# Weight parts moved 32 bytes further into their buffers in a one-core hybrid decoder layer

## The chip, the core and the metric

The kernel runs on one core of a Trainium2 chip. The time is device microseconds (us) of one execution; of the kernel before, three runs were timed. A profile of one further execution gives the rows below. Engines are named as in the profile: PE is the matrix engine's matmuls and PEld its weight loads, DVE the vector engine, ACT the scalar engine, POOL GpSimd, and SP the queue that issues the loads.

## What is computed

One layer of a decoder trunk over 256 tokens of width 2048, all in float32. The normalised tokens `xn` go through one wide input projection (22,852 columns); its columns feed four branches of width 1024. Each branch is gated, projected back to 2048 columns, weighted by a sigmoid gate and summed:

```python
[a_q, a_k, a_v, a_g, c_b, c_c, c_h, c_g, s_q, s_k, s_v, s_g, m_q, m_g,
 i_q, i_k, i_w, r_a, r_c, r_s, r_m] = [xn @ w for w in cols]
...
merged = (sigmoid(r_a) * (y_a @ w_branch[0]) + sigmoid(r_c) * (y_c @ w_branch[1])
          + sigmoid(r_s) * (y_s @ w_branch[2]) + sigmoid(r_m) * (y_m @ w_branch[3]))
return x + merged @ w_out          # and a last RMSNorm
```

The branches are a block attention, a short convolution, a sparse attention with an indexer, and an attention into 256 memory tokens. Nearly all the work is the projections: 256 tokens times some 254 MB of weights, each weight used for 256 tokens and then never again.

## The kernel before

A float32 product is made of three matmuls in the one-pass format `float32r`. Every operand is split into a rounded part `hi` and the rest `lo` (line 106: ACT casts to `hi`, DVE subtracts to get `lo`), and the product is hi·hi + hi·lo + lo·hi.

Weights arrive in 1 MB loads (`raw`, 128 partitions of 8 KB). Each load is split in two halves of 1024 columns (`split_weights`, line 117, and `quarter_parts`, line 188), and each half gets one pair of buffers `hi` and `lo` from `parts_tiles` (line 113). The pool `spl` has four buffers for `hi` and four for `lo`, used in turn, so a pair is rewritten four halves later. This is **the ring**. A buffer holds 1024 + 16 floats, 4160 bytes of each partition. 4160 is 16 times 256 plus 64, so the four buffers of a ring start 64 bytes apart modulo 256. In the addresses of the built program the ring is used in the order 0, 192, 128, 64, 0, ... bytes modulo 256 (`hi` and `lo` of a pair alike). The token tiles that meet these weights on the matrix engine (`x_hl`, `m16a`, `m16b`, `x_sums`, `y`, `mt`) all start at 0 modulo 256, and all slices of tokens and weights are multiples of 512 bytes, so a matmul's weights stand against its tokens at the ring's offset.

Two forms of matmul use the ring:

- **The 256-column form** (`products_t`, lines 141 to 143): 128 weight columns are loaded into the array (the stationary operand), and the 256 tokens stream past (the moving operand). A half of a load feeds 24 such matmuls (4 slices of k, 2 blocks of columns, 3 products).
- **The 512-column form** (`products`, lines 162 to 164): 128 tokens are loaded, and 512 weight columns stream past. A half feeds 12 such matmuls where both halves of the tokens use it (2 slices of k, 2 token halves, 3 products), and 6 where one does. The last two blocks of the output projection are 256 columns wide and also have the weights moving.

While a matmul streams its moving operand, the engine loads the stationary operand of the next one, so two streams are read from the same memory at a time. Some value and gate projections (`by_halves`, line 225) save a product of blocks by sums and differences of weight quarters, which DVE makes before the split. The order of the work is the program's own order, as a scheduler places it; nothing in it depends on an address.

Of the kernel before, what the change touches and what calls it, by code (L numbers as in the profile page):

```python
# [10 lines left out]
F32R = mybir.dt.float32r  # L11
# [4 lines left out]
P = 128  # L16
# [4 lines left out]
NB = 512  # L21
# [27 lines left out]
def hybrid_kernel(ctx, tc, x, xT, mem, memT, ln_g, mem_ln_g, w_t, w_n, w_idx, conv_w, conv_b, w_mem_k, w_mem_v,  # L49
# [7 lines left out]
    spl = ctx.enter_context(tc.tile_pool(name="spl", bufs=4))  # L57
# [53 lines left out]
        return rawp.tile([P, 4 * NB], F32, name="raw", tag="raw").rearrange("p (k c) -> p k c", c=c)  # L111

    def parts_tiles(w=NB, c=NB):
        return [spl.tile([P, 2 * NB + 16], F32R, name=n, tag=n)[:, :2 * NB].rearrange("p (k c) -> p k c", c=w)[:, :, :c]
                for n in ("hi", "lo")]

    def split_weights(src, w):

        c = src.shape[2]
        per, half = 4 * NB // w, 2 * NB // w  # L120
        for k0 in range(0, src.shape[1], per):
            raw = raw_tile(w)[:, :, :c]
            nc.sync.dma_start(out=raw, in_=src[:, k0:k0 + per])
            for h0 in range(0, per, half):
                hi, lo = parts_tiles(w, c)
                split(hi, lo, raw[:, h0:h0 + half])
                for k in range(half):
                    yield hi[:, k], lo[:, k], k0 + h0 + k
# [59 lines left out]
    def quarter_parts(raw):  # L188
        for h in (0, 2):
            hi, lo = parts_tiles()  # L190
            split(hi, lo, raw[:, h:h + 2])
            for i in range(2):
                yield hi[:, i], lo[:, i], h + i
# [131 lines left out]
    def to_heads(name, c0):  # L325

        dst = big.tile([P, 8, T], F32, name=name, tag=name)
        for b in range(4):
            copy_t(dst[:, 2 * b:2 * b + 2], project_t(w_t[FIRST[c0] + b], x_act))
        return dst  # L330
# [176 lines left out]
    def first_columns(dst):  # L507

        src = w_t[FIRST[M_Q]:FIRST[M_Q] + 2].rearrange("b p k c -> p k b c")
        outs = [bank("first", tag)[:, :T] for tag in "aabb"]  # L510
        xraw = big.tile([P, KC, T], F32, name="xraw", tag="m16b")
        for k0 in range(0, KC, 4):
            raw = raw_tile(NB).rearrange("p k (b c) -> p k b c", b=2)
            n = 1 if k0 == 0 else 2
            for k in range(k0, k0 + 4, n):
                nc.sync.dma_start(out=xraw[:, k:k + n], in_=xT[:, k:k + n])
                for i in range(n):
                    nc.sync.dma_start(out=raw[:, k + i - k0], in_=src[:, k + i])
                for i in range(n):
                    if (k + i) % 2 == 0:  # L520
                        hi, lo = parts_tiles(NB, NB)
                    split_tokens(xraw[:, k + i], k + i, g_x, x_hl[:, k + i])
                    h, lw = hi[:, (k + i) % 2], lo[:, (k + i) % 2]
                    split(h, lw, raw[:, k + i - k0].rearrange("p b c -> p (b c)"))
                    for j in range(4):
                        js = slice(j * P, (j + 1) * P)
                        products_t(outs[j], h[:, js], lw[:, js], k + i, KC, x_act)
        copy_t(dst[:, 0:4], outs)
# [40 lines left out]
    k = big.tile([P, 8, T], F32, name="kt", tag="kt")  # L569
# [28 lines left out]
    k = to_heads("kt", S_K)  # L598
# [6 lines left out]
    k = to_heads("kt", A_K)  # L605
# [111 lines left out]
```

## Time and profile before

| | |
|---|---|
| median of 3 runs | 1406.79 us (1406.69 to 1406.96) |
| profiled execution | 1407.13 us, its span in the trace 1405.4 us |
| PE busy | 1389.9 us, 99% |
| weight loads (PEld) busy | 1247.0 us, 89% |
| DVE busy | 933.1 us, 66% |
| ACT busy | 728.0 us, 52% |
| granted matrix clock | 0.999 of full speed |
| loads from HBM | 265.9 MB, mean 191 GB/s |

Matmuls are pipelined: a row's duration reaches into the next one's, so a busy share of 99% only says that something is always in flight. What a matmul costs in a row of matmuls is the distance from its start to the next one's start, which is read from the timeline. A start there is given to 0.01 us; over 12 or 24 matmuls the mean distance is known to a nanosecond.

### The profile page before, as it was taken

To read this page: it belongs to the slowest core of one execution; us is meant where nothing else is said; L and a number is where in the kernel's file an instruction comes from. 1 tells how busy PE (TensorE), PEld (TensorE's weight loads), DVE (VectorE), ACT (ScalarE), POOL (GpSimd) and SP (SyncE) were. 2 spreads that over 40 slices of the span, in tenths; PEclk is the share of its full clock that TensorE was granted. 3 is DMA by queue.
4 is the path that set the end of the run, shared out by engine and by line. 5 is a ranking of instruction groups with operands and counts; after the bars stand their busy time and mean duration, and the time that the engine had idled before them with its cause. 6 is when DMAs were issued, how large, how long until landed. Compare 5 with 4: busy or idle time off the path is not lost.

```text
span 1405.4 us, 21264 instructions
## 1 busy us (share of the span) xinstructions
PE 1389.9 (99%) x8796; PEld 1247.0 (89%) x8796; DVE 933.1 (66%) x1123; ACT 728.0 (52%) x991; POOL 11.2 (1%) x26
## 2 busy tenths in 40 slices
PE   9999999999999999999999999999999999999997
PEld 9998998779999898877999899877999998778887
DVE  6686764774757885487546886487547558787654
ACT  7664675453445585445444585445343345545443
POOL 1000000000000000000000000000000000000000
PEclk9999999999999999999999999999999999999999
DMA  9774545375553735537554645537555654736551
GB/s 343 287 260 165 206 150 180 120 269 163 187 183 121 266 128 185 197 120 243 204 184 150 239 146 188 192 114 266 200 184 182 225 194 155 265 120 240 185 200 65
DMA packets 49969, 269.49 MB, mean 192 GB/s; under 512 B 6656, under 2 KB 17456, under 8 KB 19024
## 3 DMA queue, kind: packets, MB, share of 16 engines
q1 hardware_dynamic: 48960, 264.03, 54.6%
q0 software_dynamic: 624, 3.31, 0.6%
q8 instruction: 69, 1.13, 0.3%
q10 hardware_dynamic: 288, 0.79, 0.1%
q14 instruction: 28, 0.23, 0.0%
HBM read 265.88 MB, written 2.10 MB: 191 GB/s over the span
## 4 chain that ended last, share of the span: by engine, by line
PE 85%; DVE 9%; issue 2%; DMA 2%; ACT 2%; SPq 0%; POOLq 0%; POOL 0%; DVEq 0%; ACTq 0%
PE acc L143 13%; PE acc L141 13%; PE acc L142 13%; DVE lo L108 5%; PE w L163 4%; PE w L164 4%; PE w L162 4%; PE r L163 3%; PE r L164 3%; PE r L162 3%; PE o L163 2%; PE o L162 2%; PE o L164 2%; DMA raw<-in_w_n 1%; PE y L163 1%
## 5 line engine op out<-in xcount | busy, mean ns | idle before, releaser
L108 DVE TENSOR_TENSOR lo<-raw,hi 128x1024 fp32r<-128x1024 f32 (+1 forms) x538 | 639.7, 1203 | 427.2 <-ACT hi L107 425.9
L107 ACT CAST hi<-raw 128x1024 fp32r<-128x1024 f32 (+1 forms) x538 | 550.8, 1030 | 558.0 <-PE acc L142 201.5
L142 PE MATMUL acc<-x_hl,hi 128*128 128x256 f32 x1520 | 426.5, 281 | 0.0
L143 PE MATMUL acc<-x_hl,lo 128*128 128x256 f32 x1520 | 425.9, 280 | 0.0
L141 PE MATMUL acc<-x_hl,hi 128*128 128x256 f32 x1520 | 425.3, 280 | 0.0
L141 PEld LDWEIGHTS acc<-x_hl,hi 128*128 128x128 f32 x1520 | 286.6, 189 | 0.3
L143 PEld LDWEIGHTS acc<-x_hl,lo 128*128 128x128 f32 x1520 | 286.4, 189 | 0.1
L142 PEld LDWEIGHTS acc<-x_hl,hi 128*128 128x128 f32 x1520 | 286.1, 188 | 0.3
L163 PE MATMUL w<-lo,y 128*128 128x512 f32 x256 | 100.7, 393 | 0.0
L164 PE MATMUL w<-hi,y 128*128 128x512 f32 x256 | 100.6, 393 | 0.0
L162 PE MATMUL w<-hi,y 128*128 128x512 f32 x256 | 100.6, 393 | 0.0
L163 PE MATMUL r<-lo,x_hl 128*128 128x512 f32 x248 | 97.5, 393 | 0.0
L164 PE MATMUL r<-hi,x_hl 128*128 128x512 f32 x248 | 97.4, 393 | 0.0
L162 PE MATMUL r<-hi,x_hl 128*128 128x512 f32 x248 | 97.4, 393 | 0.0
L162 PEld LDWEIGHTS w<-hi,y 128*128 128x128 f32 x256 | 48.1, 188 | 11.1
L163 PEld LDWEIGHTS w<-lo,y 128*128 128x128 f32 x256 | 48.0, 188 | 11.0
L164 PEld LDWEIGHTS w<-hi,y 128*128 128x128 f32 x256 | 48.1, 188 | 10.9
L162 PEld LDWEIGHTS r<-hi,x_hl 128*128 128x128 f32 x248 | 46.6, 188 | 10.5
L163 PEld LDWEIGHTS r<-lo,x_hl 128*128 128x128 f32 x248 | 46.5, 188 | 10.5
L164 PEld LDWEIGHTS r<-hi,x_hl 128*128 128x128 f32 x248 | 46.6, 188 | 10.4
L163 PE MATMUL o<-lo,mt 128*128 128x512 f32 (+1 forms) x160 | 55.6, 348 | 0.0
L164 PE MATMUL o<-hi,mt 128*128 128x512 f32 (+1 forms) x160 | 55.5, 348 | 0.0
(247 smaller groups left out, 1865.9 us busy)
## 6 DMA issues: line engine op xcount, KB each, us to landing
raw<-in_w_t SPq DMA_DIRECT2D x92, 1024.0 KB, 5.0
raw<-in_w_n SPq DMA_DIRECT2D x80, 1024.0 KB, 4.9
raw<-in_w_branch SPq DMA_DIRECT2D x32, 1024.0 KB, 5.2
raw<-in_w_out SPq DMA_DIRECT2D x16, 1024.0 KB, 4.8
raw<-in_w_mem_k SPq DMA_DIRECT2D x8, 1024.0 KB, 5.8
raw<-in_w_mem_v SPq DMA_DIRECT2D x8, 1024.0 KB, 4.9
raw<-in_w_t SPq DMA_DIRECT2D x16, 256.0 KB, 5.4
raw<-in_memT SPq DMA_DIRECT2D x2, 1024.0 KB, 7.6
```

Of the source, the lines that this page charges most:

```text
L107: nc.scalar.copy(out=hi, in_=src)
L108: nc.vector.tensor_sub(out=lo, in0=src, in1=hi.bitcast(F32))
L141: nc.tensor.matmul(o, lhsT=hi, rhs=a[:, 0], start=(k == 0), stop=False)
L142: nc.tensor.matmul(o, lhsT=hi, rhs=a[:, 1], start=False, stop=False)
L143: nc.tensor.matmul(o, lhsT=lo, rhs=a[:, 0], start=False, stop=(k == nk - 1))
L162: nc.tensor.matmul(o, lhsT=ah, rhs=hi, start=start, stop=False)
L163: nc.tensor.matmul(o, lhsT=ah, rhs=lo, start=False, stop=False)
L164: nc.tensor.matmul(o, lhsT=al, rhs=hi, start=False, stop=stop)
```

## The change

Each buffer of the ring keeps its size of 1024 + 16 floats, and the used part of it starts 8 floats (32 bytes) later. The four offsets modulo 256, in the order of use, become 32, 224, 160, 96. The built program has the same instructions in the same order on every engine; only addresses differ.

```diff
     def parts_tiles(w=NB, c=NB):
-        return [spl.tile([P, 2 * NB + 16], F32R, name=n, tag=n)[:, :2 * NB].rearrange("p (k c) -> p k c", c=w)[:, :, :c]
+        return [spl.tile([P, 2 * NB + 16], F32R, name=n, tag=n)[:, 8:8 + 2 * NB].rearrange("p (k c) -> p k c", c=w)[:, :, :c]
                 for n in ("hi", "lo")]
```

## Rows read from the trace of the kernel before

**Rows 1.** The page's busy time of each engine with its share of the span and its instructions, and the matrix clock in 40 slices (9 is 90% or more).
```profile
PE 1389.9 (99%) x8796; PEld 1247.0 (89%) x8796; DVE 933.1 (66%) x1123; ACT 728.0 (52%) x991; POOL 11.2 (1%) x26
...
PEclk9999999999999999999999999999999999999999
```

**Rows 2.** Groups of PE instructions, shapes apart: line, engine, operation, result<-operands, weight rows*columns, moving shape, count | busy us, mean ns | idle us before. Lines 141 and 162 only; lines 142 and 143, and 163 and 164, have as many.
```profile
L141 PE MATMUL acc<-x_hl,hi 128*128 128x256 f32 x1504 | 420.8, 280 | 0.0
...
L162 PE MATMUL w<-hi,y 128*128 128x512 f32 x256 | 100.6, 393 | 0.0
...
L162 PE MATMUL r<-hi,x_hl 128*128 128x512 f32 x248 | 97.4, 393 | 0.0
...
L162 PE MATMUL o<-hi,mt 128*128 128x512 f32 x96 | 37.7, 393 | 0.0
...
L162 PE MATMUL m<-hi,x_sums 128*128 128x512 f32 x84 | 33.7, 401 | 1.1 <-ACT hi L107 1.1
...
L162 PE MATMUL x<-hi,x_hl 128*128 128x512 f32 x84 | 33.1, 395 | 0.0
L162 PE MATMUL y<-hi,x_hl 128*128 128x512 f32 x84 | 33.1, 394 | 0.0
...
L162 PE MATMUL z<-hi,x_hl 128*128 128x512 f32 x56 | 22.2, 397 | 0.0
...
L141 PE MATMUL acc<-m16a,hi 128*128 128x256 f32 x64 | 18.0, 281 | 0.0
...
L141 PE MATMUL acc<-m16b,hi 128*128 128x256 f32 x64 | 17.8, 279 | 0.0
...
L162 PE MATMUL o<-hi,mt 128*128 128x256 f32 x64 | 17.8, 281 | 0.0
...
L141 PE MATMUL first<-x_hl,hi 128*128 128x256 f32 x64 | 16.3, 290 | 0.7 <-ACT hi L107 0.7
...
L162 PE MATMUL v<-hi,m16a 128*128 128x512 f32 x32 | 12.6, 394 | 0.0
...
L162 PE MATMUL v<-hi,m16b 128*128 128x512 f32 x32 | 12.2, 392 | 0.0
...
L162 PE MATMUL z<-hi,x_sums 128*128 128x512 f32 x28 | 11.0, 393 | 0.0
L162 PE MATMUL m<-hi,x_hl 128*128 128x512 f32 x28 | 11.0, 393 | 0.0
...
L141 PE MATMUL acc<-x_hl,hi 128*68 128x256 f32 x16 | 4.5, 278 | 0.0
```

**Rows 3.** Timeline of PE (start us, duration us) in a stretch of the 256-column form: the first matmul with each pair of the ring, at offsets 192, 128, 64, 0 and 192 again; 24 matmuls from one to the next.
```profile
392.85 0.28 PE L141 MATMUL acc<-x_hl,hi 128*128 128x256 f32 x1
...
395.57 0.28 PE L141 MATMUL acc<-x_hl,hi 128*128 128x256 f32 x1
...
398.41 0.28 PE L141 MATMUL acc<-x_hl,hi 128*128 128x256 f32 x1
...
401.15 0.28 PE L141 MATMUL acc<-x_hl,hi 128*128 128x256 f32 x1
...
404.03 0.28 PE L141 MATMUL acc<-x_hl,hi 128*128 128x256 f32 x1
```

**Rows 4.** The same in a stretch of the 512-column form: the first matmul with the pairs at 64, 0, 192, 128 and 64 again, 12 matmuls from one to the next, and between the second and the third the start of the seventh matmul of the pair at 0.
```profile
252.15 0.39 PE L162 MATMUL w<-hi,y 128*128 128x512 f32 x1
...
254.90 0.39 PE L162 MATMUL w<-hi,y 128*128 128x512 f32 x1
...
256.28 0.39 PE L162 MATMUL w<-hi,y 128*128 128x512 f32 x1
...
257.64 0.39 PE L162 MATMUL w<-hi,y 128*128 128x512 f32 x1
...
260.44 0.39 PE L162 MATMUL w<-hi,y 128*128 128x512 f32 x1
...
263.23 0.39 PE L162 MATMUL w<-hi,y 128*128 128x512 f32 x1
```

**Rows 5.** The same in the indexer's last block, where a weight load has 68 columns instead of 128: the first matmul with the pairs at 128, 64, 0 and 192, and the first of what follows; 12 matmuls from one to the next.
```profile
342.21 0.28 PE L141 MATMUL acc<-x_hl,hi 128*68 128x256 f32 x1
...
343.62 0.28 PE L141 MATMUL acc<-x_hl,hi 128*68 128x256 f32 x1
...
345.01 0.28 PE L141 MATMUL acc<-x_hl,hi 128*68 128x256 f32 x1
...
346.41 0.28 PE L141 MATMUL acc<-x_hl,hi 128*68 128x256 f32 x1
...
347.83 0.28 PE L141 MATMUL acc<-x_hl,hi 128*128 128x256 f32 x1
```

**Rows 6.** Groups that write the ring, and one that writes the token parts, shapes apart; columns as in rows 2, with what ended the idle time.
```profile
L107 ACT CAST hi<-raw 128x1024 fp32r<-128x1024 f32 x518 | 539.7, 1048 | 548.3 <-PE acc L142 195.0 <-PE w L164 98.3 <-PE r L164 74.2
...
L107 ACT CAST x_hl<-xn 128x1024 fp32r<-128x1024 f32 x4 | 4.2, 1046 | 0.0
```

**Rows 7.** The same for DVE, and the one group of matmuls that waits for it.
```profile
L108 DVE TENSOR_TENSOR lo<-raw,hi 128x1024 fp32r<-128x1024 f32 x518 | 627.3, 1224 | 414.4 <-ACT hi L107 413.2
...
L163 PE MATMUL m<-lo,x_sums 128*128 128x512 f32 x84 | 33.8, 402 | 3.0 <-DVE lo L108 3.0
```

## The prediction

> **What bounds the kernel now.** I read the page first. PE is busy for 99% of the span and its clock is granted in full in all 40 slices [rows 1]: 1389.9 us of 1405.4 us, nothing else above 89%. So the time is the number of matmuls times the distance at which one follows another, plus small stalls. The groups of PE instructions give the numbers [rows 2]. The 256-column form with the ring's weights as stationary operand counts 1504 + 16 + 64 + 64 + 64 = 1712 on line 141, and as many on lines 142 and 143: 5136. The 512-column form counts 256 + 248 + 96 + 84 + 84 + 84 + 56 + 32 + 32 + 28 + 28 = 1028 on line 162, three times that is 3084. Another 3 x 64 = 192 are the output projection's 256-column blocks with moving weights. Attention has its own buffers, which the change leaves alone. In nearly all these groups the idle time before is zero: the matmuls follow one another without a wait, and what is left is the distance from start to start.
>
> Then the timeline, one turn of the ring at a time, because the change moves addresses and nothing else. In the 256-column form [rows 3] 24 matmuls take:
> - offset 192: 395.57 - 392.85 = 2.72 us, 113.3 ns each
> - offset 128: 398.41 - 395.57 = 2.84 us, 118.3 ns
> - offset 64: 401.15 - 398.41 = 2.74 us, 114.2 ns
> - offset 0: 404.03 - 401.15 = 2.88 us, 120.0 ns
>
> The code, shapes and line numbers are the same in all four; no wait lies between. What differs is where the weights stand against the tokens, so the address has a price, up to 6.7 ns on 113.3. In the 512-column form [rows 4] 12 matmuls take 2.75 us at 64 (229.2 ns), 2.74 us at 0 (228.3), 2.80 us at 192 (233.3) and 2.79 us at 128 (232.5). The pair at 0 starts slowly and ends at (257.64 - 256.28) / 6 = 226.7 ns. The order of the offsets is another one than in the first form: 192 is best there and worst here.
>
> One view tells how far the offset alone sets the price. In the indexer's last block the weight loads are shorter, 68 columns [rows 5], and 12 matmuls take 1.41, 1.39, 1.40 and 1.42 us at 128, 64, 0 and 192: 117.5, 115.8, 116.7 and 118.3 ns. The offset 192, the best with full loads, is the worst here. So the price is not a property of the offset but of how the two streams, the moving operand and the next weights, fall against each other in time; the offset only shifts one of them.
>
> **The change part by part.** It adds and removes no instruction. Three things read or write the shifted addresses.
>
> Writes by ACT and DVE: 518 casts of 1048 ns and 518 subtractions of 1224 ns [rows 6, 7]. The nearest row with another destination is the cast into the token parts, 1046 ns [rows 6]; I take no change. They are hidden by ACT's 548 us and DVE's 414 us of idle time, which ends mostly with PE freeing a buffer. The cover is thin only where block products wait for DVE, 3.0 us in all [rows 7]; if it went there, I would expect no more than as much again, 3 us.
>
> The loads of raw weights go elsewhere and are untouched.
>
> Reads by PE. No row shows a weight part at an odd multiple of 32, so I bound it by the distances the rows show. The mean over the ring is (404.03 - 392.85) / 96 = 116.5 ns in the first form and (263.23 - 252.15) / 48 = 230.8 ns in the second.
> - First form, low end: all four at 113.3 ns, -3.1 x 5136 = -16 us. High end: all at 120.0 ns, +3.5 x 5136 = +18 us.
> - Second form, low end: 226.7 ns, -4.1 x 3084 = -13 us. High end: 233.3 ns, +2.5 x 3084 = +8 us.
> - The 192 others: at most 6.7 ns each either way, 1.3 us, taken as nothing.
>
> What I take: each new offset lies halfway between two old ones, and averaged over the ring the neighbours' means give the old mean again. That is no change, in both forms. The mix with other phases [rows 5] gives (347.83 - 342.21) / 48 = 117.1 ns, 0.6 ns over the first form's mean, +3 us. Both are mixtures of good and bad phases and I see no reason to prefer one; the middle is +1.5 us. Against the profiled execution that is 1405.4 + 1.7 around the span + 1.5 = 1408.6; that execution lies 0.3 us over the median, so **1408 us**.
>
> One rule speaks against any effect. The trace shows 113.3 and 120.0 ns for the same instructions at two addresses. The Trainium skill, page "SBUF — State Buffer", section "Who interferes with whom", states that PE reads moving operand and weights through two independent ports and never waits on anyone. By that rule the four stretches would be equal and the change worth nothing, 1406.8 us; by the rows a shift can be worth up to 30 us. The measurement decides, and the rule stays as a rival only, the last one below.
>
> **The rivals.**
>
> *Locked apart (faster).* The two streams may settle so that they no longer meet. For it: distances in a stretch settle to one value and stay there, 113.3 or 120.0 [rows 3] and 226.7 [rows 4]; all four old offsets are multiples of 64 and so meet the tokens' reads on the same 64-byte steps, and half a step may avoid them. Against it: two of the four parts in the first form are free already, and the second form reverses the order. One form alone gives 1406.8 - 16 = 1391 or 1406.8 - 13 = 1394 us; both give 1378 us. DVE would then be late next, in the block products [rows 7].
>
> *Locked together (slower).* The place is the 256-column form, lines 141 to 143. There PEld, 89% busy over the span [rows 1], has little slack beside a matmul of 256 columns, so any beat that the load loses is the matmul's loss too. 32 bytes are half of a 64-byte step: each load of 512 bytes and each moving row then begins and ends within one, and the two parts that are free now (192 and 64) lose that. The price is that of the part at 0, 120.0 ns for all four: 1406.8 + 18 = 1425 us, and with the second form at 233.3 ns 1433 us. The second form alone gives 1415 us. It decides from a ring mean of 117.0 ns on (0.55 ns x 5136 = 2.8 us). For it: every stretch off the best phase lies at 115.8 to 120 [rows 3, 5]. Against it: nothing at an odd 32 bytes was seen.
>
> *No effect.* All old offsets are multiples of 64; if the reads go in whole steps of 64 bytes, 32 bytes less than a step shift nothing, and the four stretches keep their distances in some order [rows 3]: 1406.8 us. The rule of the page named above would come to the same time.
>
> **How the numbers follow.** A measurement of this kernel can tell about 0.2%, 2.8 us, from no change. Chances: mixture as before 0.50, locked apart 0.24, locked together 0.21, no effect 0.05. The mixture can lie some 12 us to either side, since four new phases are drawn and each form's mean may move by a quarter to a half of its bounds; of its 0.50 I give 0.16 to faster, 0.16 to same and 0.18 to slower. So faster 0.16 + 0.24 = 0.40, same 0.16 + 0.05 = 0.21, slower 0.18 + 0.21 = 0.39. Cases of both signs hold most of the chance; the mixture's own range is 1396 to 1420 us. The whole range takes in either form locked alone, 1391 to 1425, and a microsecond or two for the rest: 1389 to 1427 us. Left out are both forms locked the same way, about 0.08 on each side.
>
> **What would show it.** The instruction groups must have the same counts, ACT and DVE the same mean durations to some 5 ns. In the timeline, the mean over a turn of the ring should lie within 116 to 118 ns in the first form and 229 to 232 ns in the second, with unequal stretches; equal stretches at 113.3 or 120.0 would show one of the locked cases, and the sum of both forms' shifts must give the change of the total to a few microseconds. I am wrong if PE's waits, DVE's times or the clock change instead, or if the ring means leave the bounds of [rows 3, 4].

## The result, and the profile after

The changed kernel takes 1417.97 us, median of 3 runs (1417.93 to 1419.27), against 1406.79 us before: a ratio of 1.0082, 95% interval 1.0059 to 1.0105. It is **slower by 11.2 us**. The profiled execution took 1417.97 us; its span is 1416.2 us, 10.8 us more than before.

The page's busy times and the matrix clock, as in [rows 1]:

```profile
PE 1402.0 (99%) x8796; PEld 1253.9 (89%) x8796; DVE 933.8 (66%) x1123; ACT 728.3 (51%) x991; POOL 11.2 (1%) x26
...
PEclk9999999999999999999999999999999999999999
```

PE is busy for 12 us more; DVE, ACT and the clock stayed. The instruction counts are the same. So the matmuls follow one another at larger distances, and the timeline of PE says where. The first matmul with each pair of the ring in the stretch of [rows 3], now at offsets 224, 160, 96, 32 and 224 again, 24 matmuls apart:

```profile
395.37 0.28 PE L141 MATMUL acc<-x_hl,hi 128*128 128x256 f32 x1
...
398.18 0.28 PE L141 MATMUL acc<-x_hl,hi 128*128 128x256 f32 x1
...
401.05 0.28 PE L141 MATMUL acc<-x_hl,hi 128*128 128x256 f32 x1
...
403.87 0.28 PE L141 MATMUL acc<-x_hl,hi 128*128 128x256 f32 x1
...
406.70 0.28 PE L141 MATMUL acc<-x_hl,hi 128*128 128x256 f32 x1
```

The differences are 2.81, 2.87, 2.82 and 2.83 us: 117.1, 119.6, 117.5 and 117.9 ns for a matmul, where before they were 113.3, 118.3, 114.2 and 120.0. The worst stretch hardly changed; what went are the two stretches at 113 and 114 ns. The same for the 512-column form of [rows 4], at offsets 96, 32, 224, 160 and 96 again, 12 matmuls apart:

```profile
253.77 0.40 PE L162 MATMUL w<-hi,y 128*128 128x512 f32 x1
...
256.58 0.39 PE L162 MATMUL w<-hi,y 128*128 128x512 f32 x1
...
259.38 0.39 PE L162 MATMUL w<-hi,y 128*128 128x512 f32 x1
...
262.17 0.40 PE L162 MATMUL w<-hi,y 128*128 128x512 f32 x1
...
264.98 0.40 PE L162 MATMUL w<-hi,y 128*128 128x512 f32 x1
```

2.81, 2.80, 2.79 and 2.81 us: 234.2, 233.3, 232.5 and 234.2 ns. All four now lie within 1 ns of the dearest one before (233.3).

These are single stretches. To add them up I took the start distance of each of the 5136 and 3084 matmuls from the trace and set aside those more than 25 ns above 113.3 or 226.7 ns (44 and 51 of them before) as waits. The means of the others over the ring, and what the waits take beyond these means:

| | before | after | difference | times count |
|---|---|---|---|---|
| 256-column form | 116.75 ns | 118.04 ns | +1.29 ns | +6.6 us |
| its waits | 6.0 us | 5.3 us | | -0.7 us |
| 512-column form | 231.21 ns | 233.39 ns | +2.18 ns | +6.7 us |
| its waits | 11.4 us | 9.9 us | | -1.5 us |
| sum | | | | +11.1 us |

The span grew by 10.8 us, so nothing else is left to explain. The waits fell a little. In the 512-column form, those that end with a cast of ACT or a subtraction of DVE took 8.5 us before and 7.3 us now, which fits a slower PE that gives these engines more time (the group of [rows 7] waits 2.8 us instead of 3.0); for the rest of the fall the profile names no releaser. The writers of the ring kept their durations, answering to [rows 6, 7]; the groups of ACT and of DVE:

```profile
L107 ACT CAST hi<-raw 128x1024 fp32r<-128x1024 f32 x518 | 540.2, 1048 | 556.6 <-PE acc L142 201.6 <-PE w L164 100.0 <-PE r L164 75.4
...
L108 DVE TENSOR_TENSOR lo<-raw,hi 128x1024 fp32r<-128x1024 f32 x518 | 627.4, 1224 | 423.2 <-ACT hi L107 421.6
```

Both idle 8 to 9 us longer, ACT mostly until PE frees a buffer and DVE until ACT's cast. They are not the cause.

### The profile page after: what moved, and what is told of

It reads as the page before. It is cut to its first block, busy times and chain, and to the rows that moved or that the text cites. A ratio compares the mean times of both kernels' runs of the same rounds, so it can differ in the third digit from the quotient of the medians.

```text
span 1416.2 us, 21264 instructions
## 1 busy us (share of the span) xinstructions
PE 1402.0 (99%) x8796; PEld 1253.9 (89%) x8796; DVE 933.8 (66%) x1123; ACT 728.3 (51%) x991; POOL 11.2 (1%) x26
## 4 chain that ended last, share of the span: by engine, by line
PE 88%; DVE 7%; issue 2%; ACT 2%; DMA 1%; SPq 0%; POOLq 0%; POOL 0%; DVEq 0%; ACTq 0%
PE acc L143 13%; PE acc L141 13%; PE acc L142 13%; DVE lo L108 4%; PE w L164 4%; PE w L163 4%; PE w L162 4%; PE r L164 4%; PE r L162 4%; PE r L163 4%; PE o L163 2%; PE o L162 2%; PE o L164 2%; PE y L163 1%; PE y L164 1%
## 5 line engine op out<-in xcount | busy, mean ns | idle before, releaser
L162 PEld LDWEIGHTS w<-hi,y 128*128 128x128 f32 x256 | 48.1, 188 | 11.4
L162 PE MATMUL o<-hi,mt 128*128 128x512 f32 (+1 forms) x160 | 55.9, 350 | 0.0
L164 PE MATMUL o<-hi,mt 128*128 128x512 f32 (+1 forms) x160 | 55.8, 350 | 0.0
```

The source lines that it names most:

```text
L162: nc.tensor.matmul(o, lhsT=ah, rhs=hi, start=start, stop=False)
L164: nc.tensor.matmul(o, lhsT=al, rhs=hi, start=False, stop=stop)
```

## The experiments

Theory: a matmul's distance goes by the difference of address between the weight parts and the tokens, modulo 256, and none of 32, 96, 160, 224 is cheap. Rivals: the parts' own addresses count; or the price comes from the hand-over from one offset to the next; or one form causes all of it by way of waits. The order of PE's instructions is that of the kernel before in all of these kernels. Ratios are to runs of the kernel before on the same chip (1406.2 to 1406.4 us).

### Own address or difference: e1, e2

e1 moves everything that lies behind one constant tile by 32 bytes, tokens and parts alike, by making that tile longer:

```diff
-    fill = const.tile([P, 56], F32, name="fill")
+    fill = const.tile([P, 64], F32, name="fill")
```

> The kernel before with everything behind one constant tile (tokens and weight parts alike) 32 bytes further: absolute addresses of the weight parts as in the change (32, 96, 160, 224 modulo 256), difference to the tokens as before (0, 64, 128, 192). Theory 'difference': the price of a matmul goes by weights minus tokens, so 1406.8 us, ring means 116.7 and 231.2 ns, and single stretches at 113.3 ns again. Rival 'own address': a part that starts at an odd multiple of 32 bytes costs more by itself, so about 1418 us, ring means 118.0 and 233.4 ns as in the change.

Measured: 1406.61 us, ratio 1.0002 (0.9993 to 1.0011). Ring means 116.75 and 231.20 ns, each offset at the price that the same difference had before. PE in the stretch of [rows 3], with the parts at 192, 128, 64, 0 and 192 from the tokens as there:

```profile
392.39 0.28 PE L141 MATMUL acc<-x_hl,hi 128*128 128x256 f32 x1
...
395.11 0.28 PE L141 MATMUL acc<-x_hl,hi 128*128 128x256 f32 x1
...
397.95 0.28 PE L141 MATMUL acc<-x_hl,hi 128*128 128x256 f32 x1
...
400.69 0.28 PE L141 MATMUL acc<-x_hl,hi 128*128 128x256 f32 x1
...
403.57 0.28 PE L141 MATMUL acc<-x_hl,hi 128*128 128x256 f32 x1
```

The differences are 2.72, 2.84, 2.74 and 2.88 us, those of [rows 3].

e2 moves the tokens 32 bytes down, and with them the other buffers ahead of the ring (raw loads, attention's buffers), and keeps the parts in place by an unused tile ahead of the ring. Of the two operands of the ring's matmuls, only the tokens move:

```diff
-    fill = const.tile([P, 56], F32, name="fill")
+    fill = const.tile([P, 48], F32, name="fill")
...
+    gap = ctx.enter_context(tc.tile_pool(name="gap", bufs=1))
     spl = ctx.enter_context(tc.tile_pool(name="spl", bufs=4))
...
+    space = gap.tile([P, 8], F32, name="space")
+    nc.gpsimd.memset(space, 0.0)
```

> The kernel before with the tokens 32 bytes earlier and the weight parts where they were: difference 32, 96, 160, 224 as in the change, the parts' own addresses as before. 'Difference': about 1418 us, ring means 118.0 and 233.4 ns. 'Own address': 1406.8 us if only the parts' addresses count. If any operand off 64 bytes costs by itself, e1 would be the slowest of all and this about like the change.

Measured: 1418.32 us, ratio 1.0085 (1.0070 to 1.0100); ring means 118.04 and 233.36 ns, those of the change to 0.03 ns. PE in the same stretch, with the parts at 32, 224, 160, 96, 32 and 224 from the tokens (line 144 here is line 141 of the kernel before):

```profile
392.89 0.28 PE L144 MATMUL acc<-x_hl,hi 128*128 128x256 f32 x1
...
395.72 0.28 PE L144 MATMUL acc<-x_hl,hi 128*128 128x256 f32 x1
...
398.53 0.28 PE L144 MATMUL acc<-x_hl,hi 128*128 128x256 f32 x1
...
401.40 0.28 PE L144 MATMUL acc<-x_hl,hi 128*128 128x256 f32 x1
...
404.22 0.28 PE L144 MATMUL acc<-x_hl,hi 128*128 128x256 f32 x1
...
407.05 0.28 PE L144 MATMUL acc<-x_hl,hi 128*128 128x256 f32 x1
```

From the second start on the differences are 2.81, 2.87, 2.82 and 2.83 us, those of the changed kernel. So the same prices come with the parts where they were before (e2) and 32 bytes further on (the change): where they lie makes no difference, only their distance from the tokens. The rival of the own address has fallen, and with it the idea that half a 64-byte step costs something by itself.

### One form alone: e8, e9

`parts_tiles` is told which form asks, and starts at 8 floats for one form and at 0 for the other (e8: the parts that are loaded are shifted; e9: those that stream). The rest of each line is left out at `rearrange(...)`:

```diff
-    def parts_tiles(w=NB, c=NB):
+    def parts_tiles(w=NB, c=NB, stream=True):
+        s = 0 if stream else 8            # e9: 8 if stream else 0
-        return [spl.tile([P, 2 * NB + 16], F32R, name=n, tag=n)[:, :2 * NB].rearrange(...)
+        return [spl.tile([P, 2 * NB + 16], F32R, name=n, tag=n)[:, s:s + 2 * NB].rearrange(...)
```

> The change for the 256-column form alone, in the buffers of before; the parts that stream stay at 0, 64, 128, 192. If the two forms' terms add: (118.04 - 116.75) x 5136 = +6.6 us, 1413 us, and 231.2 ns in the other form. If the slower time comes from one form only by way of waits, 1406 or 1418 us.

> The change for the parts that stream alone (512-column form and the output projection's 256-column blocks); the parts that are loaded stay at 0, 64, 128, 192, in the buffers of before. If the two forms' terms add: (233.39 - 231.21) x 3084 = +6.7 us, less the 1.5 us of waits for DVE that went in the change, so 1411.5 us, and 116.7 ns in the other form. If the forms act on each other where one follows the other, the sum of this one and of the 256-column form alone (+6.1 us measured) misses the change's +11.2 us by more than 1 us.

Measured: e8 1412.39 us, ratio 1.0045 (1.0028 to 1.0062), +6.1 us; means 118.02 and 231.17 ns. e9 1411.59 us, ratio 1.0037 (1.0023 to 1.0051), +5.2 us. The sum, 11.3 us, is the change's 11.2 us. The two forms' terms add, and each is worth about half.

### One offset for the whole ring: e3, e4, e7

Buffers of exactly 1024 floats put all four pairs at the same offset modulo 256; a tile of 0, 16 or 8 floats ahead of the ring sets it to 0, 64 or 32 bytes:

```diff
-        return [spl.tile([P, 2 * NB + 16], F32R, name=n, tag=n)[:, :2 * NB].rearrange(...)
+        return [spl.tile([P, 2 * NB], F32R, name=n, tag=n)[:, :2 * NB].rearrange(...)
...
+    space = gap.tile([P, 16], F32, name="space")      # e4; 8 floats in e7, no tile in e3
```

> Buffers of 1024 floats without the 16 spare ones, so that all four pairs of the ring stand at offset 0 and no stretch hands over to another offset. Theory 'offset sets the price': the 256-column form at 120.0 ns, (120.0 - 116.75) x 5136 = +16.7 us; the 512-column form at 226.7 ns as at the end of its stretch before, (226.7 - 231.2) x 3084 = -13.9 us; 1409.6 us together. Rival 'hand-over': the price comes from the change of offset between stretches, then both forms fall to their low values, 113.3 and 226.7 ns, about 1375 us.

Measured: 1413.49 us, ratio 1.0052 (1.0037 to 1.0067). The means are 119.90 and 227.09 ns, close to 120.0 and 226.7; the hand-over theory, which wanted 113.3 in the first form, has fallen there. In the second form a part of the price is the hand-over's: at offset 0 the ring of before has a mean of 229.5 ns, and held at 0 the same form has 227.1. PE in e3, two starts 12 apart, 2.72 us or 226.7 ns each:

```profile
256.12 0.39 PE L162 MATMUL w<-hi,y 128*128 128x512 f32 x1
...
258.84 0.39 PE L162 MATMUL w<-hi,y 128*128 128x512 f32 x1
```

The total is 4 us over the expected sum mainly because the waits in the 512-column form rose from 11.4 to 15.8 us. Of these 4.4 us, 2.3 end with a cast of ACT or a subtraction of DVE, so a faster PE waits for them; for the rest the profile names no releaser.

> The same with all four pairs at offset 64. 'Offset sets the price': 113.3 ns, -17.7 us, and 229.0 ns, (229.0 - 231.2) x 3084 = -6.8 us; 1382 us. A rival on the same side: at offset 64 the trace of before shows stretches that stay at 117.7 ns, so the phase that is found at the start may hold all through; then +4.9 - 6.8, about 1405 us. 'Hand-over': about 1375 us as at offset 0.

Measured: 1394.90 us, ratio 0.9915 (0.9895 to 0.9935), between the two times expected, and the four runs spread from 1391.25 to 1397.45 us. The 512-column form has 229.05 ns. The 256-column form has a mean of 115.40 ns, and the timeline shows why it is a mean of two values. PE in two stretches of e4, two starts 24 matmuls apart in each (line 144 here is line 141 of the kernel before):

```profile
732.65 0.28 PE L144 MATMUL acc<-x_hl,hi 128*128 128x256 f32 x1
...
735.37 0.28 PE L144 MATMUL acc<-x_hl,hi 128*128 128x256 f32 x1
...
1068.36 0.28 PE L144 MATMUL acc<-x_hl,hi 128*128 128x256 f32 x1
...
1071.18 0.28 PE L144 MATMUL acc<-x_hl,hi 128*128 128x256 f32 x1
```

2.72 us is 113.3 ns each, 2.82 us is 117.5; more exactly, 113.3 holds for all sets of 24 from 667 to 746 us, and 117.8 for all from 984 to 1159 us. The code is the same, the offset is the same, and no wait lies within either stretch. In the addresses of the built program, the 96 pairs of slices (weights and tokens) that run at 113.3 ns between 360 and 432 us are the same that run at 117.8 after 984 us, and each writes to the same banks of PSUM, the matrix engine's result memory: **there are two states, and in this trace the one that is found in the first set of a long run of matmuls is kept to the run's end.** One run of 1536 matmuls in the other state would change the time by some 7 us, an estimate from the two prices; the four executions lie 6.2 us apart. Whether the states are what sets them apart is not shown, since one execution was profiled.

> All four pairs at offset 32. 'Offset sets the price', with the mean of the stretches at 32 in the change (118.1 and 232.9 ns): +1.3 x 5136 + 1.7 x 3084 = 12 us, 1418 us. Rival 'half a step has a free state too, and the ring's hand-overs keep it from being found': 113.3 and 226.7 ns, about 1380 us.

Measured: 1418.98 us, ratio 1.0091 (1.0076 to 1.0106); 118.29 and 233.30 ns. The timeline of PE in e7, two starts 24 apart:

```profile
395.95 0.28 PE L144 MATMUL acc<-x_hl,hi 128*128 128x256 f32 x1
...
398.79 0.28 PE L144 MATMUL acc<-x_hl,hi 128*128 128x256 f32 x1
```

2.84 us, 118.3 ns, and so, to 0.4 ns, for every set of 24 of the long runs. With half a step held for the whole kernel, no stretch at 113.3 or 226.7 ns was seen. The rival that the ring's hand-overs keep it from being found has fallen, at 32; the offsets 96, 160 and 224 were only run in turn.

### An offset for each form: e5, e6

The kernel before and e3 say that parts that stream are best at 0; the kernel before and e4 say that parts that are loaded are best at 192 or 64. Room for buffers of 1024 + 64 floats comes from the indexer's `score`, which is kept in a temporary buffer:

```diff
-        score = const.tile([P, 384], F32, name="score")
+        score = tmp.tile([P, 512], F32, name="pr")[:, :384]
...
+        s = 0 if stream else 48                              # e5
+        s = 0 if stream else (48, 16)[next(calls) % 2]       # e6: 192 and 64 bytes in turn
+        return [spl.tile([P, 2 * NB + 64], F32R, name=n, tag=n)[:, s:s + 2 * NB].rearrange(...)
```

> An offset for each form, in buffers of 1024 + 64 floats (room for them comes from keeping the indexer's score in a temporary buffer): weight parts that are loaded (256-column form) at 192, parts that stream (512-column form) at 0. Theory 'offset sets the price, with two states at the free offsets': 512 columns at 226.7 ns, -4.2 x 3084 = -13 us, of which block products that wait for DVE give back some 4 us as at offset 0 in all buffers; 256 columns at 113.3 ns if the free state holds, -3.4 x 5136 = -17 us, about 1380 us; if both states share it as at 64 (115.4 ns), -7 us, about 1390 us. Rival 'one stretch's gain is lost elsewhere' (waits for DVE or loads grow as PE gets faster): about 1395 us or more.

Measured: 1401.15 us, ratio 0.9960 (0.9947 to 0.9973), 11 to 21 us over the two times of the theory. It lies in the range of the rival (1395 us or more), but not by the rival's mechanism: the waits of both forms are only 2.8 us longer than before. The 512-column form is at 227.09 ns as expected. The 256-column form is at 117.33 ns on average, because here five of the six long runs fell into the dear state and stayed there (the sixth, of 192 matmuls, ran at 113.3). PE in e5, two starts 24 apart (line 142 is line 141 of before):

```profile
1068.07 0.28 PE L142 MATMUL acc<-x_hl,hi 128*128 128x256 f32 x1
...
1070.89 0.28 PE L142 MATMUL acc<-x_hl,hi 128*128 128x256 f32 x1
```

2.82 us again. In the kernel before, stretches at the same offset 192 ran at 113.3 [rows 3].

> The same, but the parts that are loaded stand at 192 and 64 in turn. If handing over from one free offset to the other makes the streams find the free state again, all stretches lie at 113.5 to 114.2 ns and the time at about 1381 us, with little spread between executions. If the hand-over only costs its first matmuls (10 to 22 cycles of them at the step to 64 before), about 1385 us. If it throws them into the dear state, 117.7 ns, about 1403 us.

Measured: **1385.84 us, ratio 0.9854 (0.9839 to 0.9869), the fastest version**, faster than both kernels; its runs lie within 1384.63 to 1386.21 us. PE in e6 at offsets 64, 192, 64, 192, 64 (line 144 is line 141 of before):

```profile
385.94 0.28 PE L144 MATMUL acc<-x_hl,hi 128*128 128x256 f32 x1
...
388.66 0.28 PE L144 MATMUL acc<-x_hl,hi 128*128 128x256 f32 x1
...
391.38 0.28 PE L144 MATMUL acc<-x_hl,hi 128*128 128x256 f32 x1
...
394.10 0.28 PE L144 MATMUL acc<-x_hl,hi 128*128 128x256 f32 x1
...
396.82 0.28 PE L144 MATMUL acc<-x_hl,hi 128*128 128x256 f32 x1
```

Four times 2.72 us. With a step of offset every 24 matmuls the long runs that begin dear (117.6 to 118.0 ns for one to three sets) come back to 113.3 and stay; the mean of all is 114.28 ns. Half of these sets stand at the offset 64, with the same weights that e4 ran at 117.8 after 984 us, so the values of the weights do not decide the state. So stepping between two offsets that have a cheap state is not an average of them, but a way back into that state. The sum, (114.28 - 116.75) x 5136 + (227.10 - 231.21) x 3084 + 2.2 us of waits = -23.2 us, stands against -22.6 us between the spans of the two profiled executions (1382.8 against 1405.4) and -20.4 us in the median.

## Why the prediction was right or wrong

**What bounds the kernel**: right. PE's start distances times the counts of [rows 2] give +11.1 us where the span grew by 10.8; the clock, DVE and ACT did not move.

**Writes and loads cost nothing**: right. The cast and the subtraction kept 1048 and 1224 ns.

**No change, since each new offset lies between two old ones**: this step failed, and it is where the forecast of 1408 us went wrong. Price is not a straight line between neighbours. In the first form the dear end moved little (120.0 before, 119.6 now in the same stretch) and the cheap end vanished: 113.3 to 117.1. In the second form all four went to the dear end, 233.4 ns, outside the 229 to 232 that I gave for a mixture, and just over the 233.3 that I had set as the form's upper bound, past which I said I would be wrong. The middle of +1.5 us was +11.2 us: +6.6 us from the first form and +6.7 from the second, less some 2 us of waits. The measured time lies in the mixture's own range of 1396 to 1420 us and in the whole range, but by the width of the mixture, not by its reasoning: that is luck.

**The 68-column rows as a sample of other phases** [rows 5]: they pointed the right way (117.1 ns, +3 us) and were too low by half; full loads came to 118.0. That block itself, 117.1 before, is at 116.5 now ((350.07 - 344.48) / 48), so it is no sample for the others. The block of the changed kernel at offsets 160, 96, 32 and 224:

```profile
344.48 0.28 PE L141 MATMUL acc<-x_hl,hi 128*68 128x256 f32 x1
...
345.88 0.28 PE L141 MATMUL acc<-x_hl,hi 128*68 128x256 f32 x1
...
347.27 0.28 PE L141 MATMUL acc<-x_hl,hi 128*68 128x256 f32 x1
...
348.68 0.28 PE L141 MATMUL acc<-x_hl,hi 128*68 128x256 f32 x1
...
350.07 0.28 PE L141 MATMUL acc<-x_hl,hi 128*128 128x256 f32 x1
```

What I took from those rows, that the offset alone does not set the price, is borne out by the two states of e4 and e5; that it is set by how the two streams fall against each other in time stays an argument.

**Locked apart**: did not happen; at 32 no cheap state was seen (e7). **Locked together**: its sign and its deciding point, a ring mean over 117.0 ns, were right, and its 233.3 ns for the second form too. Its price for the first form, 120.0 ns, was too high by 2 ns, and its reason is wrong: e1 moves all operands to odd multiples of 32 and costs nothing.

**No effect**: fell with the result. The rule of the Trainium skill, page "SBUF — State Buffer", section "Who interferes with whom", that PE never waits on anyone, does not foresee this, and the measurement decides: of these matmuls' operands e2 moves the tokens alone, by 32 bytes, and the kernel takes 12 us longer; e1 moves both, and it takes the same time. The runs show that the price depends on where the two operands stand to each other; they do not show by what part of the chip.

Still open: why the price has these values, and what decides which state a run of matmuls starts in.

## What to carry to other kernels

When a kernel is bound by PE with few waits left, compare the start distances of like matmuls whose operands lie at different addresses: here they differed by 6% with nothing else changed. Place the operand that is loaded and the one that streams with their difference modulo 256 in mind, for each form of matmul by itself, and where a cheap state is found at two offsets, try stepping between them: here that brought the cheap state back (e6). The offsets at multiples of 64 did not tell the prices of those between them; an average over neighbours is not a forecast.

## What the runs showed of the hardware

Mean start distance in ns of float32r matmuls, waits set aside, by weight part minus tokens modulo 256; for 0, 32, 64 and 192 the offset was held for the whole kernel (192 in the 256-column form only), the others are from rings that step, and the 115.4 and 117.3 are mixtures of two states in one execution:

| offset | 0 | 32 | 64 | 96 | 128 | 160 | 192 | 224 |
|---|---|---|---|---|---|---|---|---|
| loaded, 256 columns stream | 119.9 | 118.3 | 115.4 | 117.6 | 118.4 | 119.6 | 117.3 | 116.9 |
| streams, 512 columns | 227.1 | 233.3 | 229.1 | 233.9 | 232.4 | 233.7 | 233.2 | 233.1 |

At 64 and at 192, held for the whole kernel, the 256-column form has two states, 113.3 and 117.8 ns. In the traces the cheap one was kept for up to 87 us (e4, from 665 us) and the dear one for up to 181 us (e4, from 984 us; e5, from 989 us), each to the end of its run. The lowest values, 113.3 and 226.7 ns, are 0.443 ns a column at a granted clock of 0.999 of 2.4 GHz, 6% more than one column a cycle; no offset that was tried had a lower mean.
